# Placing every operand tile and the identity matrix at multiples of 256 bytes in a hybrid encoder kernel

## The chip, the core and the metric

The kernel runs on one core of one Trainium2 chip. The metric is the device time of one launch in microseconds (us), as the median of the runs shown. The engines are called PE (TensorE matmul), PEld (its weight loads), DVE (VectorE), ACT (ScalarE), POOL (GpSimd) and SP (SyncE, which issues the DMAs).

## The reference

One layer of an encoder trunk, run for two batches with the same weights: a prompt of 512 tokens and a sample of 1024 tokens, model width 1024, all in fp32.

```
def _trunk(x, ...):
    h = _rmsnorm(x, norm_attn_g)
    z = h @ w_in                                   # q, k, v, ca, cb
    a_out = _window_attn(q, k, v, bias, band, sink)  # 8 heads of 64, 2 kv heads, |q-k| <= 128
    c = ca * jax.nn.sigmoid(cb)
    c = _dwconv(c, conv_dw_w, conv_dw_b)           # 31 taps, centred, 512 channels
    c = jax.nn.silu(_layernorm(c, conv_ln_g, conv_ln_b))
    x = x + jnp.concatenate([a_out, c], axis=-1) @ w_out
    h = _rmsnorm(x, norm_ffn_g)
    u = _dwconv(h @ w_up, ffn_dw_w, ffn_dw_b)      # 3 taps, 2 * 2816 channels
    x = x + (jax.nn.silu(u[..., :D_FF]) * u[..., D_FF:]) @ w_down
    return _rmsnorm(x, norm_final_g)
```

## The kernel before

**The arithmetic.** Each fp32 operand of a large product is split into a high part in fp32r (the format that PE streams) and a low part, the remainder. A product is then three matmuls into the same PSUM bank: high times high, high times low, low times high. These are the triples of lines L250, L251 and L253 (`proj`, projections by `w_in` and the prompt's up projection), L638 to L640 (`out_half`, output projection), L810 to L812 (down projection of the prompt), L1042 to L1044 (`prod`, up projection of the sample) and L1351 to L1353 (`mm_down`, down projection of the sample). Nearly all have 512 moving columns. The sample's feed-forward part is written as a Strassen-like scheme of seven block products. L501 are the attention scores, with 256 or 384 columns. L175, L184, L209, L354, L543, L602, L614 and L965 are transposes on PE: data as the stationary operand, the identity matrix `ident` as the moving one (L184 transposes the identity itself, to keep PE active at the start).

**The stages.** Up to about 370 us: projections by `w_in` for prompt and sample, with attention and the depthwise convolution beside them. Then, to about 830 us, the prompt's feed-forward part, with the sample's attention and the rest of its convolution beside it. Then the sample's output projection and transposes, from about 910 us its up projection, and from about 1340 us its down projection and the final norm.

**Memory.** SBUF is given out by a class `Slots`: named slots of fixed sizes, each a tile of a pool with the slot's name as its tag, taken by the smallest size that fits and returned when the holder is dropped. Class q has 15 slots of 4096 bytes per partition, h 61 of 2048, c 4 of 4224, d 2 of 2176, s 32 of 64 (statistics and scalars, of which an instruction uses a few columns). A slot gets its address when it is first used, one behind the other; so an s slot taken between two h slots moves all that follow. Ahead of them lie the constants: `ident`, `nhalf`, `warm`, `vecs` (norm weights and biases as columns), `rs2`, `cvw` and `fw` (taps), `sinkb`, `nsink`, `rb`.

```
        fits = [s for s in self.free if s[1] >= need and (among is None or s[0][0] in among)]
        ...
        least = min(s[1] for s in fits)
        slot = next(s for s in fits if s[1] == least)
```

The addresses modulo 256 that come of it in the kernel before (an address is the byte offset within a partition; columns within a tile start at multiples of 512 bytes from it, for all large matmuls):

| tiles | count | address modulo 256, before | after |
|---|---|---|---|
| q (raw weights, split weights, rows of x) | 15 | 160 | 0 |
| h (high and low parts, 512 columns) | 61 | 160 (48), 32 (7), 96 (3), 224 (3) | 0 |
| c (padded rows of the sample, later split weights) | 4 | 32 (3), 160 (1) | 0 |
| d (padded rows of the prompt) | 2 | 160, 224 | 0 |
| ident | 1 | 128 | 0 |
| vecs | 1 | 192 | 0 |
| s | 32 | all multiples of 32 | all multiples of 32 |

Of the 6069 matmuls with 512 columns in fp32r, 4179 have both operands at 160; by stage the share is 77 to 89% up to 800 us and 53 to 61% after it.

**What sets the order.** A scheduler orders the instructions up to the sample's feed-forward part; from there PE's order, and at the end SP's too, is the order of the code. The convolution (L293, `conv_items`) reads its padded input at a shift of one column, 4 bytes, per tap: 24 to 27 taps on DVE, the others as products on ACT and sums on POOL.

Of the kernel before, what the change touches and what calls it, by code (L numbers as in the profile page):

```python
# [9 lines left out]
F32 = mybir.dt.float32  # L10
# [5 lines left out]
P = 128  # L16
# [4 lines left out]
NH = 8  # L21
# [5 lines left out]
PAD = CK // 2  # L27
# [69 lines left out]
def tile_hybrid_encoder(ctx: ExitStack, tc: tile.TileContext, xs, rel_bias, norm_attn_g, w_in,  # L97
                        attn_sink, conv_dw_w, conv_dw_b, conv_ln_g, conv_ln_b, w_out, norm_ffn_g,
                        w_up, ffn_dw_w, ffn_dw_b, w_down, norm_final_g, onehot, outs):
    nc = tc.nc  # L100
    cst = ctx.enter_context(tc.tile_pool(name="cst", bufs=1))
    big = ctx.enter_context(tc.tile_pool(name="big", bufs=1))
    dr = ctx.enter_context(tc.tile_pool(name="dr", bufs=1, space=bass.MemoryType.DRAM))
    ps_guards = [tc.tile_pool(name=f"ps{i}", bufs=1, space=bass.MemoryType.PSUM) for i in range(4)]
    ps = [guard.__enter__() for guard in ps_guards]
    two_of = dict(a0=0, a1=0, a2=1, u0=1, u1=2, b0=2, b1=3, c0=3)

    sb = Slots(big, dict(q=(15, 4096), c=(4, 4224), h=(61, 2048), d=(2, 2176), s=(32, 64)))
    banks = Slots(lambda tag: ps[two_of[tag]], dict(a=(3, 2048), u=(2, 2048), b=(2, 2048), c=(1, 2048)))
    use = dict(step="aub", turn="aub", conv="c", attn="au", norm="b", out="b", up="u", down="b")  # L110

# [3 lines left out]
    def bank(job):  # L115
        return banks.tile([NT], among=use[job])

    GR = [dict(g=0, nN=1, nb=4, x=xs[0], o=outs[0], T=512), dict(g=1, nN=2, nb=8, x=xs[1], o=outs[1], T=1024)]

    ident = cst.tile([P, P], F32, name="ident")  # L120
    nhalf = cst.tile([P, 1], F32, name="nhalf")
    nc.gpsimd.memset(nhalf[:], -0.5)
    warm = cst.tile([P, 1], F32, name="warm")
    nc.scalar.activation(warm[:], nhalf[:], AF.Exp)

    def rstd_of(ss, n, out):
# [41 lines left out]
    def rows_T(parts, out):  # L168
        r = sb.tile([P])
        n = 0  # L170
        for src, k in parts:
            nc.sync.dma_start(r[n:n + k, :], src)
            n += k
        pt = bank("step")
        nc.tensor.transpose(pt[:, :n], r[:n, :], ident[:n, :n])  # L175
        nc.vector.tensor_copy(out, pt[:, :n])

    rw = lambda v: v.rearrange("o (k p) -> (o k) p", p=P)
    vecs = cst.tile([P, 72], F32, name="vecs")
    rows_T([(rw(norm_attn_g), 8)], vecs[:, 0:8])  # L180
    for _ in range(NW // 4):
        pt = bank("step")
# [125 lines left out]
    def evac(kind, c, nt, src):  # L308
        g, n = (0, 0) if nt == 0 else (1, nt - 1)
        T = GR[g]["T"]  # L310
        cols = slice(n * NT, (n + 1) * NT)
        if kind == "cb":
            t = sb.tile([NT])
            nc.scalar.activation(t[:], src, AF.Tanh, scale=0.5)
            tanh_t[nt, c] = t
        elif kind == "ca":
            if n == 0:
                cp = sb.tile([T + 2 * PAD])
                nc.gpsimd.memset(cp[:, 0:PAD], 0.0)
                nc.gpsimd.memset(cp[:, PAD + T:2 * PAD + T], 0.0)  # L320
                cpads[g, c] = cp
            cp = cpads[g, c]
            nc.vector.scalar_tensor_tensor(cp[:, PAD + n * NT:PAD + (n + 1) * NT], tanh_t.pop((nt, c))[:], 1.0, src,  # L323
                                           op0=ALU.add, op1=ALU.mult)
        elif kind == "q":
            hi, lo = sb.tile([NT], F32R), sb.tile([NT], F32R)
            nc.scalar.activation(hi[:], src, AF.Identity, scale=QSCALE)
            nc.vector.scalar_tensor_tensor(lo[:], src, QSCALE, hi[:].bitcast(F32),
                                           op0=ALU.mult, op1=ALU.subtract)
            for e in range(2):  # L330
                for L, s in ((0, hi), (1, lo)):
                    nc.sync.dma_start(
                        qsd[nt][:, L * HD:(L + 1) * HD, 2 * c + e, :].rearrange("b p t -> p b t"),
                        s[e * HD:(e + 1) * HD, :].bitcast(F32).rearrange("p (b t) -> p b t", t=P))
        elif kind == "k":
            hi, lo = sb.tile([NT], F32R), sb.tile([NT], F32R)
            nc.scalar.copy(hi[:], src)
            nc.vector.tensor_tensor(lo[:], src, hi[:].bitcast(F32), op=ALU.subtract)
            for kv in range(NKV):
                if g == 0:  # L340
                    kt[0, kv] = [sb.tile([T], F32R) for _ in range(2)]
                for L, s in ((0, hi), (1, lo)):
                    src_k = s[kv * HD:(kv + 1) * HD, :].bitcast(F32)
                    if g == 0:
                        for half in range(2):
                            nc.sync.dma_start(kt[0, kv][L][half * HD:(half + 1) * HD, :].bitcast(F32), src_k)
                    else:
                        nc.sync.dma_start(ksd[:, kv, L, cols], src_k)
        else:
            vs = sb.tile([NT])  # L350
            nc.scalar.copy(vs[:], src)
            pt = bank("step")
            for i in range(4):
                nc.tensor.transpose(pt[:, i * P:(i + 1) * P], vs[:, i * P:(i + 1) * P], ident[:])  # L354
            src = pt[:].rearrange("p (b c) -> p b c", c=P)
            vs = []
            for kv in range(NKV):
                v = sb.tile([4, P], F32R)
                head = slice(kv * HD, (kv + 1) * HD)
                rest = slice((1 - kv) * HD, (2 - kv) * HD)  # L360
                nc.scalar.copy(v[:, :, head], src[:, :, head])
                nc.vector.tensor_tensor(v[:, :, rest], src[:, :, head], v[:, :, head].bitcast(F32), op=ALU.subtract)
                if g == 1:
                    nc.sync.dma_start(vsd[:, n, kv], v[:].bitcast(F32))
                vs.append(v)
            if g == 0:
                vt[0] = vs
# [16 lines left out]
    def step(i, nt):  # L384
        kind, c, col = order[i]
        pp = bank("step")
        proj(pp[:], ws[i], h1[nt], i < 2 and nt == 0)
        evac(kind, c, nt, pp[:])
        if kind == "ca" and nt != 1:
            g = 0 if nt == 0 else 1  # L390
            (convs, late)[g].append(conv_items(g, c, cpads.pop((g, c))))
        tick()
# [10 lines left out]

    cvw = cst.tile([P, CK * 4], F32, name="cvw")
    fw = cst.tile([P, 132], F32, name="fw")
    sinkb = cst.tile([P, NH], F32, name="sinkb")
    nsink = cst.tile([P, NH], F32, name="nsink")

    def constants():
        rows_T([(rw(norm_ffn_g), 8), (rw(conv_dw_b), 4), (rw(conv_ln_g), 4), (rw(conv_ln_b), 4),  # L410
# [1156 lines left out]
```

## Time and profile before

| | |
|---|---|
| median of 3 runs | 1574.7 us (1574.6 to 1577.9) |
| span of the profiled execution | 1572.4 us (the page gives no other time for it) |
| PE busy | 1526.1 us, 97% |
| PEld busy | 1239.3 us, 79% |
| DVE busy | 1180.7 us, 75% |
| ACT, POOL busy | 801.3 us, 745.2 us |
| mean granted clock of PE | 0.992 |
| DMA | 207.62 MB, 42% of 16 engines |

Busy time of PE is the union of its matmuls. They overlap: the record of one lasts some 393 ns, while the next starts some 230 ns after it. So the pace of matmuls is read from one start to the next, or from the count of weight loads (one for each matmul) in a window in which PE does not idle. In the views, a line of the timeline gives start and duration in us, engine, line, operation, tiles (written <- read, buffer numbers left out: h is any h slot, w, u, a, b are PSUM banks) and shapes. A line of a tile or source view gives the count, then minimum/median/maximum in ns. A line of waits gives who waited for whom, us in total, times, and the longest in us.

### The profile page before, as it was taken

How to read it: one execution, taken by the hardware profiler on the slowest of the kernel's cores; microseconds unless marked ns; L12 is line 12 of the kernel's file. 1: busy time of each engine (PE TensorE's matmuls, PEld its weight loads, DVE VectorE, ACT ScalarE, POOL GpSimd, SP SyncE). 2: the span in 40 equal slices, each digit the busy share in tenths (PEclk: the TensorE clock that was granted, in tenths of full speed). 3: DMA queues.
4: the chain of work that ended last, by engine and by line, in shares of the span. 5: the costliest groups of instructions: out<-in, count | busy, mean ns of one | idle time of the engine just before them, and what ended most of it. 6: DMA issues, size and time to landing. Idle time of an engine off the chain costs nothing. (4 is left out here: it accounts for less than half of the span.)

```text
span 1572.4 us, 20204 instructions
## 1 busy us (share of the span) xinstructions
PE 1526.1 (97%) x6909; PEld 1239.3 (79%) x6909; DVE 1180.7 (75%) x1659; ACT 801.3 (51%) x1402; POOL 745.2 (47%) x655
## 2 busy tenths in 40 slices
PE   8999898998999999999999999999999999999998
PEld 6788777886878877888778887888888878788886
DVE  7999757647869996657575777777787777877794
ACT  4635654335466665655554354454444445554364
POOL 7652334317677777556562333555555454000235
PEclk9999999999999999999999999999999999999999
DMA  7583244427333233323658132333333332594642
GB/s 227 158 207 98 74 121 115 146 78 211 108 103 106 83 118 105 110 88 110 182 156 269 54 94 75 100 100 101 101 100 102 100 114 88 201 367 142 220 142 107
DMA packets 209771, 207.62 MB, mean 132 GB/s; under 512 B 11156, under 2 KB 150748, under 8 KB 209541
## 3 DMA queue, kind: packets, MB, share of 16 engines
q1 hardware_dynamic: 209669, 206.35, 42.0%
q8 instruction: 54, 0.88, 0.2%
q14 instruction: 48, 0.39, 0.1%
HBM read 158.84 MB, written 48.51 MB: 132 GB/s over the span
## 5 line engine op out<-in xcount | busy, mean ns | idle before, releaser
L144 POOL TENSOR_TENSOR q<-q,q 128x1024 fp32r<-128x1024 f32 x72 | 174.7, 2430 | 85.1 <-ACT q L143 51.7
L918 POOL TENSOR_TENSOR q<-q,q 128x512 fp32r<-128x512 f32 x82 | 115.0, 1413 | 155.9 <-ACT q L1028 152.4
L251 PE MATMUL u<-h,q 128*128 128x512 f32 x400 | 159.0, 398 | 0.4 <-DVE h L212 0.4
L250 PE MATMUL u<-h,q 128*128 128x512 f32 x400 | 158.2, 396 | 1.0 <-DVE h L212 0.9
L253 PE MATMUL u<-h,q 128*128 128x512 f32 x384 | 152.2, 397 | 1.1 <-POOL q L144 1.1
L1042 PE MATMUL w<-h,q 128*128 128x512 f32 x372 | 147.4, 396 | 2.5 <-ACT h L1123 1.5
L1044 PE MATMUL w<-h,q 128*128 128x512 f32 x372 | 145.6, 392 | 0.6 <-POOL q L918 0.6
L293 DVE SCALAR_TENSOR_TENSOR c<-c,cvw,c 128x512 f32<-128x512 f32 x184 | 138.0, 750 | 2.7
L1043 PE MATMUL w<-h,q 128*128 128x512 f32 x350 | 137.7, 393 | 0.0
L143 ACT CAST q<-q 128x1024 fp32r<-128x1024 f32 x72 | 75.6, 1050 | 101.3 <-POOL q L144 46.7
L915 POOL TENSOR_TENSOR q<-q,q 128x1024 f32<-128x1024 f32 x8 | 23.9, 2999 | 181.7 <-DVE q L915 170.4
L250 PE MATMUL b<-h,q 128*128 128x512 f32 x256 | 102.8, 402 | 4.4 <-DVE d L323 2.9
L1351 PE MATMUL w<-h,h 128*128 128x512 f32 x264 | 103.7, 393 | 0.0
L1353 PE MATMUL w<-h,h 128*128 128x512 f32 x264 | 103.6, 392 | 0.0
L253 PE MATMUL b<-h,q 128*128 128x512 f32 x256 | 102.0, 399 | 0.9 <-POOL q L144 0.9
L251 PE MATMUL b<-h,q 128*128 128x512 f32 x256 | 102.0, 399 | 0.0
L918 DVE TENSOR_TENSOR h<-h,h 128x512 fp32r<-128x512 f32 (+1 forms) x128 | 92.3, 763 | 11.4 <-ACT h L922 8.7
L918 POOL TENSOR_TENSOR c<-q,c 128x512 fp32r<-128x512 f32 x46 | 71.9, 1576 | 50.9 <-ACT c L1028 50.9
L1352 PE MATMUL w<-h,h 128*128 128x512 f32 x244 | 95.9, 393 | 0.0
L250 PEld LDWEIGHTS u<-h,q 128*128 128x128 f32 x400 | 75.8, 189 | 17.8 <-DVE h L212 1.1
L251 PEld LDWEIGHTS u<-h,q 128*128 128x128 f32 x400 | 75.7, 189 | 17.1 <-DVE h L212 2.2
L922 ACT CAST h<-h 128x512 fp32r<-128x512 f32 x101 | 59.1, 619 | 57.8 <-DVE h L918 23.6
(456 smaller groups left out, 4275.0 us busy)
## 6 DMA issues: line engine op xcount, KB each, us to landing
q<-in_w_up SPq DMA_DIRECT2D x88, 512.0 KB
h<-in_w_down SPq DMA_DIRECT2D x90, 256.0 KB
ga<-q SPq DMA_DIRECT2D x64, 256.0 KB
h<-ga SPq DMA_DIRECT2D x57, 256.0 KB
q<-in_w_in SPq DMA_DIRECT2D x28, 512.0 KB
q<-in_x_sample SPq DMA_DIRECT2D x15, 512.0 KB
h<-qsd SPq DMA_DIRECT2D x24, 256.0 KB
q<-ga SPq DMA_DIRECT2D x20, 256.0 KB
```

The source lines that it names most:

```text
L144: (nc.vector if dve else nc.gpsimd).tensor_tensor(lo[:], raw[:], hi[:].bitcast(F32), op=ALU.subtract)
L250: nc.tensor.matmul(out, whi[:, kc, :], hi[:], start=(kc == 0), stop=False)
L251: nc.tensor.matmul(out, whi[:, kc, :], lo[:], start=False, stop=False)
L253: nc.tensor.matmul(out, wlo[:, kc, :], hi[:], start=False, stop=(kc == KC - 1))
L293: nc.vector.scalar_tensor_tensor(acc[:], src(t), w(t), acc[:], op0=ALU.mult, op1=ALU.add)
L918: (eng or nc.vector).tensor_tensor(out, a, b, op=ALU.subtract)
L1042: nc.tensor.matmul(out, whi[:, s], hi[:], start=(start and c == 0), stop=False, **go)
L1043: nc.tensor.matmul(out, whi[:, s], lo[:], start=False, stop=False, **go)
L1044: nc.tensor.matmul(out, wlo[:, s], hi[:], start=False, stop=(stop and c == 3), **go)
L1351: nc.tensor.matmul(out, sh[:, c], th[:], start=(p == 0), stop=False)
L1352: nc.tensor.matmul(out, sh[:, c], tl[:], start=False, stop=False)
L1353: nc.tensor.matmul(out, sl[:, c], th[:], start=False, stop=(p == NPAIR - 1))
```

## The change

Three things, all in the placing of SBUF tiles:

- The s slots get a pool of their own, `sml`, ahead of the pool of the large slots, so that no small slot lies between large ones.
- The sizes of the c and d slots grow from 4224 to 4352 and from 2176 to 2304 bytes, multiples of 256; the padded rows of the convolution are asked for with 64 columns beyond their tokens instead of 30. `vecs` grows from 72 to 96 columns.
- `nhalf`, `warm`, `sinkb` and `nsink` are declared ahead of `ident`, so that the constants ahead of it fill up to a multiple of 256.

```
+    sml = ctx.enter_context(tc.tile_pool(name="sml", bufs=1))
     big = ctx.enter_context(tc.tile_pool(name="big", bufs=1))
...
-    sb = Slots(big, dict(q=(15, 4096), c=(4, 4224), h=(61, 2048), d=(2, 2176), s=(32, 64)))
+    sb = Slots(lambda tag: sml if tag[0] == "s" else big,
+               dict(q=(15, 4096), c=(4, 4352), h=(61, 2048), d=(2, 2304), s=(32, 64)))
...
+    nhalf = cst.tile([P, 1], F32, name="nhalf")
+    warm = cst.tile([P, 1], F32, name="warm")
+    sinkb = cst.tile([P, NH], F32, name="sinkb")
+    nsink = cst.tile([P, NH], F32, name="nsink")
     ident = cst.tile([P, P], F32, name="ident")
-    nhalf = cst.tile([P, 1], F32, name="nhalf")
...
-    warm = cst.tile([P, 1], F32, name="warm")
...
-    vecs = cst.tile([P, 72], F32, name="vecs")
+    vecs = cst.tile([P, 96], F32, name="vecs")
...
-                cp = sb.tile([T + 2 * PAD])
+                cp = sb.tile([T + 64])
...
-    sinkb = cst.tile([P, NH], F32, name="sinkb")
-    nsink = cst.tile([P, NH], F32, name="nsink")
```

On each of the five engines the program of the change has the same instructions in the same order with the same waits, and each tile sits in the slot of the same name. Only the addresses differ, as the table above gives them.

## The prediction

> **What bounds the kernel now.** I read the page first (busy time, slices, chain), then the windows of 200 us, then the timeline of PE matmul by matmul, then the waits of PE, and last the views of single lines and tiles. The page:
>
> ```profile
> span 1572.4 us, 20204 instructions
> PE 1526.1 (97%) x6909; PEld 1239.3 (79%) x6909; DVE 1180.7 (75%) x1659; ACT 801.3 (51%) x1402; POOL 745.2 (47%) x655
> DVE  7999757647869996657575777777787777877794
> PEclk9999999999999999999999999999999999999999
> PE 34%; DVE 2%; DMA 1%; ACT 1%; issue 0%; POOL 0%; SPq 0%; POOLq 0%; DVEq 0%; ACTq 0%
> q1 hardware_dynamic: 209669, 206.35, 42.0%
> ```
>
> PE is the bound: 1526.1 of 1572.4 us, at the full granted clock, and PE leads the chain. So 46.3 us at most are PE's idle time; the rest is the pace of its matmuls. DVE is nearly full in 7 of the 40 slices (the nines), elsewhere it has room. The profile's page has no time of its own beside the span; the median of the runs, 1574.7, is 2.3 us above the span, and I carry these 2.3 us along. About 0.2% (3 us) is what a measurement here can tell from no change.
>
> An address enters the kernel's time only where an instruction's duration depends on it, since the program of the change has the same instructions, waits and slots in the same order. So the question is which durations depend on addresses. The first is the pace of matmuls with 512 columns, 6069 of the 6909. Three windows (columns: length, then busy us and count of PE, PEld, DVE, ACT, POOL, then clock, DMA share, GB/s):
>
> ```profile
> 94.72:105.61 10.89, 10.89 (x50) 9.01 (x48) 9.72 (x15) 4.12 (x7) 4.95 (x3) 1.00 0.80 184
> 1476.76:1487.87 11.11, 11.11 (x49) 9.02 (x48) 8.40 (x9) 4.99 (x9) 3.36 (x2) 1.00 0.61 196
> 1000.00:1200.00 200.00, 200.00 (x866) 162.00 (x865) 155.23 (x145) 97.32 (x142) 106.45 (x72) 1.00 0.30 99
> ```
>
> PE never idles in any of them, and the weight loads count the matmuls: 10.89/48 = 226.9 ns each in the first, 11.11/48 = 231.5 ns in the second, 200/865 = 231.2 ns in the third. By the slot table, all 48 matmuls of the first have both operands at 160 modulo 256, but only 12 of the 48 in the second. The first has the busier DMA and DVE, so contention is not the reason. Over the whole trace I took the interval from each 512-column matmul's start to the next start, where its neighbours on both sides have 512 columns too and the interval is below 250 ns: 2600 whose own and neighbours' operands all lie at 160 (first and last in the first two rows below) average 228.9 ns, the other 3005 (last two rows) 231.5 ns. All 5847 intervals below 250 ns average 230.4 ns.
>
> ```profile
> 17.81 0.39 PE L251 MATMUL u<-h,q 128*128 128x512 f32 x1
> 1561.31 0.39 PE L1352 MATMUL w<-h,h 128*128 128x512 f32 x1
> 115.58 0.39 PE L253 MATMUL b<-h,q 128*128 128x512 f32 x1
> 1564.33 0.39 PE L1353 MATMUL w<-h,h 128*128 128x512 f32 x1
> ```
>
> **The change part by part.**
>
> *Operand tiles to one residue.* It is the only term of size. The mixture of residues 160, 224, 32 and 96 becomes 0 everywhere. If only equality counts, each matmul moves to the pace of the uniform ones. Lower end: 228.9, the mean with equal direct neighbours, gives (230.4 - 228.9) x 5847 = 8.8 us. Upper end: 226.9, the first window's, gives 3.5 x 5847 = 20.5 us. I take 227.8, midway between the two, since long equal stretches are what the change makes but even these are broken by transposes and waits: 2.6 x 5847 = 15.2 us of PE time.
>
> Not all of it reaches the end. Where DVE is full, PE would only wait more:
>
> ```profile
> 40.00:80.00 40.00, 36.27 (x184) 29.59 (x183) 39.27 (x55) 24.54 (x37) 26.47 (x24) 0.96 0.52 155
> 0.00:200.00 200.00, 184.10 (x879) 149.86 (x880) 173.34 (x283) 101.40 (x187) 99.56 (x114) 0.98 0.52 152
> ```
>
> From 40 to 80 us DVE is busy for 39.27 of 40. The nines are 7 of 40 slices, 17% of the span; but there the share of uniform matmuls is already 77 to 89% (0 to 600 us) against 53 to 61% after 800 us, where PE never idles and DVE has 155 of 200. So less than a fifth of the saving lies in those slices. I let 13 of 15.2 us pass (85%), ends 6.8 (0.77 of 8.8) and 19 (0.93 of 20.5). What is late next there is DVE, with its products for PE.
>
> *Identity matrix, from 128 to 0 modulo 256.* Weight loads of the identity itself and of data tiles at 160, both for transposes:
>
> ```profile
> L184 PEld LDWEIGHTS a<-ident x20: 139/142/230, 1.5 to 9.6; 128*128 128x128 f32 x20
> L209 PEld LDWEIGHTS a<-ident,q x80: 138/141/231, 9.7 to 367.4; 128*128 128x128 f32 x80
> ```
>
> Medians 142 and 141 ns: nothing to gain. On the moving side the identity feeds 640 transposes of 128 columns; at the 2.6 ns above that is 1.7 us, the upper end, and 0 the lower. I take 0, by the rows; the work is on PE, and nothing hides it.
>
> *DVE, ACT and POOL operands.* The depthwise convolution reads its input at every shift of 4 bytes (tap t of L293 starts 4t bytes further), a natural trial of alignment:
>
> ```profile
> L293 DVE SCALAR_TENSOR_TENSOR c<-c,cvw,c x184: 725/750/757, 181.2 to 599.2; 128x512 f32<-128x512 f32 x184
> L293 DVE SCALAR_TENSOR_TENSOR c<-d,cvw,c x78: 735/756/757, 41.4 to 169.9; 128x512 f32<-128x512 f32 x78
> ```
>
> Minimum and maximum are 4% apart over all shifts: no alignment matters to DVE. I take 0 for the three engines, by these rows; the ends are 1% of the time of the slices in which DVE is full, 0.01 x 275 = 3 us either way.
>
> *DMA, small slots, padding, moved declarations.* The same bytes move in the same packets. PE waits on DMA little in all:
>
> ```profile
> PE u L501 <- DMA h<-qsd: 2.8, 2, 2.4
> PE a L501 <- DMA q<-ksd: 2.5, 1, 2.5
> PE a L602 <- DMA h<-cvd: 1.1, 1, 1.1
> ```
>
> That is 6.4 us. Shorter packets could take back a tenth of it, 0.6 us; DMA is at 42%, so PE's own backlog hides the rest. I take 0, ends -1 and +1. The small slots hold scalars and statistics, and keep their width of 64 bytes; the padding and the order of declarations issue nothing.
>
> Sum: 1572.4 - 13 = 1559.4 span, plus 2.3 = 1561.7, so 1562 us.
>
> **The rivals.**
>
> *A larger gain: the whole fixed part of a matmul goes.* In scores with 256 columns four matmuls follow each other at once:
>
> ```profile
> 728.95 0.64 PE L501 MATMUL a<-q,h 128*128 128x256 f32 x4
> 729.43 0.40 PE L250 MATMUL u<-h,q 128*128 128x512 f32 x1
> ```
>
> Start to start it is 0.48 us for 4, 120 ns each. With 226.9 ns for 512 columns that makes 0.4176 ns a column and 13.1 ns that do not scale. Every fp32r operand of the kernel starts 32 bytes off a multiple of 64. If the 13.1 ns is one more read for an operand that begins inside a line, it goes at residue 0: 213.8 ns a matmul, 16.6 x 5847 = 97 us of PE time. PE would then leave DVE behind in more places (DVE 1180.7 of some 1480), so I let 0.7 pass: 68 us, 1507 us; with half of the 13.1 ns gone, some 1530. For it: the fixed part is the same at both lengths. Against: it may belong to the change of weights, and no operand at a multiple of 64 and full rate exists in the trace. The Trainium skill, "TensorE: Matmul & The Clock Gate", section Back-to-back issue gap, gives N / 2.4 + 2.5 ns, 215.8 ns for 512 columns; by that page this rival's pace is the normal one, while no window here is below 226.9 ns.
>
> *No change.* The residue is a mark of the stage and not the cause, or 0 is as mixed as before because a higher part of the address counts. Then 1574.7, between 1572 and 1577. Against: in each of the eight windows of 200 us the uniform ones of the intervals counted above are the faster, by 0.9 to 3.7 ns; for: the 0.9 and 1.1 ns fall between 1000 and 1400 us, where most is to be had, and 296 of the 2600 uniform ones still take 235 to 237 ns. The Trainium skill, "SBUF — State Buffer", section Specifications (TRN2), speaks for this rival: lines are 16 bytes, and every operand before starts at a multiple of 32, so nothing could be gained; the two windows above speak against it.
>
> *Slower: weights and moving operand collide from the first byte.* PE loads the next weights while it streams, and with everything at 0 both reads could begin in the same part of memory. The price is the step seen within uniform matmuls, from 226.9 to 236 ns: (236 - 230.4) x 5847 = 33 us, 1607 us; it decides once more than 4 in 10 matmuls take that step ((230.4 - 226.9)/9.1). Against: with both at 160 they begin equally close today, and that stretch is the fastest.
>
> **How the numbers follow.** Forecast (uniform pace): 0.46, own range 1552 to 1572 (1574.7 less 19 and 6.8 us, with 1 us for DMA and 3 us for DVE). Larger gain: 0.26, 1490 to 1545 around 1507. No change: 0.16. Slower: 0.12. The range 1505 to 1577 leaves out the lower half of the larger gain (0.13) and the slower cases above 1577 (0.07). Faster by over 0.2%: 0.46 + 0.26, 0.72 in all; within 0.2%: 0.15; slower: 0.13.
>
> **What would show it.** In the trace after, the window from 1000 to 1200 us should hold about 878 weight loads (200/0.2278) instead of 865; 930 would mean the larger gain, 865 no change, 850 or less the collision. L293 should keep 750 to 756 ns, L184 and L209 their 141. PE's idle time should grow by 2 us or so, ended by DVE. I am wrong if the pace stays mixed with equal residues, or if the pace improves and the span does not, which would put the bound on DVE over more than its nine slices.

## The result and the profile after

The change makes the kernel faster: 1556.8 us median (1554.4 to 1557.6, 4 runs) against 1576.3 (1574.6 to 1579.4, 4 runs) of the kernel before, a ratio of 0.9878 with a 95% interval of 0.9859 to 0.9898. The forecast was 1562 us, with 1552 to 1572 as the likeliest case's own range. In a later session the same kernel gave 1559.2 us and 0.9901 [0.9884, 0.9917].

The page of the kernel after (lines of the code are 4 further for L1xx to L3xx and 2 further behind them, so L293 is now L297):

```profile
span 1554.2 us, 20204 instructions
PE 1508.0 (97%) x6909; PEld 1236.7 (80%) x6909; DVE 1179.0 (76%) x1659; ACT 799.6 (51%) x1402; POOL 743.5 (48%) x655
DVE  7999857647979996657575767777787877887795
q1 hardware_dynamic: 209669, 206.35, 41.5%
DVE 0%; issue 0%; POOLq 0%; POOL 0%; ACT 0%
```

PE is still the bound. Its busy time fell by 18.1 us (1526.1 to 1508.0) and the span by 18.2 us; what lies between them, PE's idle time, is 46.2 us as before. The chain of waits broke off in the last microseconds and tells nothing here, so the windows have to do. The window from 1000 to 1200 us, and the slice in which DVE was fullest:

```profile
1000.00:1200.00 200.00, 199.80 (x877) 163.90 (x876) 159.61 (x149) 97.87 (x146) 109.99 (x73) 1.00 0.32 105
40.00:80.00 40.00, 34.90 (x184) 28.21 (x183) 39.38 (x56) 24.44 (x37) 26.53 (x24) 1.00 0.50 156
```

876 weight loads stand in the first where 865 stood. In the second nothing is gained: 183 weight loads in both kernels, since DVE is busy for 39.38 of 40 us. From start to start, the 5849 intervals of 512-column matmuls below 250 ns average 227.6 ns (before: 5847 at 230.4), and 4769 of them last 226 or 227 ns (before: 1805). Setting the same interval of both traces side by side, in PE's order, splits the gain: those that changed by less than 25 ns give 16.4 us, those that changed by more 2.6 us. The latter are waits, and matmuls in short stretches in which the granted clock was 0.50 (multiples of some 3.4 us; the window from 40 to 80 us, at 0.96 before and 1.00 after, held one before). PE worked 18.6 us at this half clock before and 11.9 us after, which is an estimated 3 us of its busy time. These stretches differ between executions of one kernel: a second trace of the kernel after has 18.0 us of them, at the same span of 1554.2 us. So the trace puts nearly all of the gain into the pace. The experiments show that this is only half of the story.

The other rows that the prediction went by: DVE's convolution, the transposes' weight loads, and PE's waits on DMA.

```profile
L297 DVE SCALAR_TENSOR_TENSOR c<-c,cvw,c x184: 720/750/757, 180.6 to 593.6; 128x512 f32<-128x512 f32 x184
L188 PEld LDWEIGHTS a<-ident x20: 139/142/231, 1.5 to 9.5; 128*128 128x128 f32 x20
L213 PEld LDWEIGHTS a<-ident,q x80: 138/140/144, 9.6 to 365.9; 128*128 128x128 f32 x80
PE u L503 <- DMA h<-qsd: 2.9, 1, 2.9
PE a L604 <- DMA h<-cvd: 1.5, 1, 1.5
PE a L503 <- DMA q<-ksd: 0.9, 1, 0.9
```

750 ns and 142 and 140 ns are the medians of before within 1 ns; PE's waits on DMA went from 6.4 to 5.3 us.

### The profile page after: what moved, and what is told of

It reads as the page before. It is cut to its first block, busy times and chain, and to the rows that moved or that the text cites. A ratio compares the mean times of both kernels' runs of the same rounds, so it can differ in the third digit from the quotient of the medians.

```text
span 1554.2 us, 20204 instructions
## 1 busy us (share of the span) xinstructions
PE 1508.0 (97%) x6909; PEld 1236.7 (80%) x6909; DVE 1179.0 (76%) x1659; ACT 799.6 (51%) x1402; POOL 743.5 (48%) x655
## 3 DMA queue, kind: packets, MB, share of 16 engines
q1 hardware_dynamic: 209669, 206.35, 41.5%
## 5 line engine op out<-in xcount | busy, mean ns | idle before, releaser
L1044 PE MATMUL w<-h,q 128*128 128x512 f32 x372 | 146.3, 393 | 3.3 <-ACT h L1125 1.9
L297 DVE SCALAR_TENSOR_TENSOR c<-c,cvw,c 128x512 f32<-128x512 f32 x184 | 138.0, 750 | 2.7
```

The costliest lines, as they stand in the source:

```text
L297: nc.vector.scalar_tensor_tensor(acc[:], src(t), w(t), acc[:], op0=ALU.mult, op1=ALU.add)
L1044: nc.tensor.matmul(out, whi[:, s], hi[:], start=(start and c == 0), stop=False, **go)
```

## The experiments

**Theories.** E: what counts is that the operands of successive matmuls share a residue, whichever. Z: residue 0 itself counts. And, once E stood: where the waits come from that a common residue other than 0 brings.

**1. Matmuls by themselves.** A kernel of groups of 96 matmuls back to back, each with its own weights, 24 moving operands and 12 weights in turn, at chosen residues:

```
+    ("m160", 512, mv(160), z),            # name, columns, moving residues, weights' residues (z: all 0)
+    ("m0_64", 512, mv(0, 64), z),
+            nc.tensor.matmul(pt[:, :n], W[:, b:b + P], M[:, a:a + n], start=(k == 0), stop=(k == NMM - 1))
```

> A kernel of its own: 30 groups of 96 back-to-back matmuls, each with its own weight load, their operands' addresses chosen group by group; it computes nothing of the reference's, and its time isn't compared with it, only the interval from one matmul's start to the next, read group by group. Theory E (what counts is that successive moving operands start at the same place within an address period): 226.7 ns for 512 columns in every group in which all moving operands share a residue, whether it is 0, 16 or 160; groups in which they alternate between 0 and 64 mod 256 cost some 10 ns more a matmul (a single operand off by 64 cost about 20 ns in two steps in the trace of before), those between 0 and 128 some 3 ns more (6 ns in two steps). Theory Z (residue 0 itself is what is fast): 226.7 ns at 0 alone and 230 ns or more in the group at 160. Theory S (the weights' addresses count as much as the moving operand's): the groups that alternate the stationary operand between 0 and 64 cost 5 to 10 ns more, too; if not, only the moving side counts. 256 and 384 columns at equal residues: 120.0 and 173.3 ns. If some sequence of residues falls below 226.7 ns, there is a faster layout than the change's.

Windows of 70 matmuls within a group (the first column behind the window is its length, 70 intervals). In this order, with 512 columns: moving 160 and weights 0; moving 0 and weights 160; both 160; moving alternating 0 and 64, weights 0; both 0:

```profile
47.10:63.50 16.40, 16.40 (x71) 13.19 (x70) 0.00 (x0) 0.00 (x0) 0.00 (x0) 1.00 0.00 0
69.57:85.90 16.33, 16.33 (x71) 13.14 (x70) 0.00 (x0) 0.00 (x0) 0.00 (x0) 1.00 0.00 0
91.85:107.72 15.87, 15.87 (x71) 13.14 (x70) 0.00 (x0) 0.00 (x0) 0.00 (x0) 1.00 0.00 1
135.98:152.19 16.21, 16.21 (x71) 13.13 (x70) 0.00 (x0) 0.00 (x0) 0.00 (x0) 1.00 0.00 0
514.11:529.98 15.87, 15.87 (x72) 13.14 (x71) 0.00 (x0) 0.00 (x0) 0.00 (x0) 1.00 0.00 0
```

16.40/70 = 234.3 ns, 233.3, 226.7, 231.6, 226.7. For the pace, Z is refuted: both at 160 is as fast as both at 0. E holds, with a sharper edge than it had: in the first two groups no operand deviates from its predecessor of the same kind, and they are among the slowest. It is the weights and the moving operand that must share the residue, not only moving operands among themselves. By group means, moving operands alternating between 0 and another residue, with weights at 0, cost 5.0 ns a matmul at 32 and 64, 3.3 at 96, 128 and 224, 6.7 at 160 and nothing at 192; weights alternating between 0 and 64 cost 3.4 ns. So equality is not the whole rule: alternating with 192 is unequal in half of the pairs and costs nothing. My 10 ns for a step by 64 was too much, the 3 ns for 128 right. No group of 512 columns falls below 226.7 ns.

**2. All tiles at 160.** The changed kernel with wider `vecs`, which pushes all slots (not `ident`) 160 bytes on:

```
-    vecs = cst.tile([P, 96], F32, name="vecs")
+    vecs = cst.tile([P, 136], F32, name="vecs")
```

> The changed kernel with every operand tile (not the identity) 160 bytes further: all at 160 mod 256. Theory E (equal residues count, whichever): within 0.2% of the changed kernel, 1554 to 1560 us, ratio to before 0.988; the 512-column interval stays at 227.6 ns. Theory Z (residue 0 counts): back to about 1575 us, ratio 1.0, interval 230 ns.

Measured: 1566.6 us, ratio 0.9931 [0.9915, 0.9947], between the two expectations. Its page, and the window from 1000 to 1200 us:

```profile
span 1564.9 us, 20204 instructions
PE 1511.4 (97%) x6909; PEld 1239.0 (79%) x6909; DVE 1178.4 (75%) x1659; ACT 799.1 (51%) x1402; POOL 739.8 (47%) x655
q1 hardware_dynamic: 209669, 206.35, 42.3%
1000.00:1200.00 200.00, 198.29 (x870) 162.62 (x869) 156.88 (x146) 98.15 (x144) 103.34 (x71) 1.00 0.32 102
```

The pace is 227.64 ns, that of the changed kernel, so E is right about the pace inside the kernel, too. But PE idles for 53.5 us instead of 46.2: the time that the pace gives is partly lost in waits. Set beside the changed kernel interval by interval, small differences sum to 0.4 us and large ones to 9.2 us; they are scattered over stage changes and DMA waits, the largest 1.2 us (ahead of L559, at 769 us).

**3 and 4. Half of the tiles 64 or 128 bytes off.** Filler between slots h35 and h36 (64 shown, or 128):

```
         self.free.remove(slot)
+        if slot[0] == "h36" and not self.fill:
+            self.fill = self.pool("h36").tile([P, 64 // 4], F32, tag="fill", name="fill", bufs=1)
```

> The changed kernel with 64 bytes of filler ahead of slot h36, so that h36 to h60 and c lie at 64 mod 256 and all else at 0. Of the 6070 matmuls with 512 columns 1980 (before: 1956, of which 1111 by 64 and 845 by 128) follow one whose moving operand lies at the other residue. Theory E with a dear 64-byte step: 1980 steps at 10 to 13 ns = 20 to 26 us more than the changed kernel, 1576 to 1583 us, so as slow as before or slower, ratio 1.000 to 1.005. If a period of 64 bytes is all that counts: 1557 us, ratio 0.988.

> As the run with half the tiles 64 bytes off, with 128 bytes of filler: the same 1980 steps, now between 0 and 128 mod 256. If 128 bytes is the period that counts: 1557 us, ratio 0.988. If steps by 128 cost the 3 ns that single deviating operands cost in before's trace: 1980 x 3 = 6 us, 1562 us, ratio 0.991. If a step by 128 costs what one by 64 does: 1576 to 1583 us, ratio 1.000 to 1.005.

Measured: 1571.3 us, ratio 0.9973 [0.9957, 0.9988], and 1571.0 us, 0.9968 [0.9953, 0.9982]. The pace is 230.97 and 230.62 ns, 3.4 and 3.0 ns above the changed kernel: spread over the 1980 steps, 10 and 9 ns each. The 10 ns for a step by 64 holds, the 3 ns for one by 128 does not: a step by 128 costs nearly the same, so neither 64 nor 128 bytes is the period. After experiment 1 the count to take is another: by the slots' addresses, weights and moving operand lie at different residues in some 1810 of the 512-column matmuls of the kernel before, 2350 in each of these two, and 1200 in experiment 8. The loss of pace against the changed kernel is 9.0, 8.4, 7.5 and 7.6 ns for each of them. Not only they lose: the prediction's 2600 matmuls with equal operands in themselves and their direct neighbours took 228.9 ns, not 227.6, which suggests that an unequal pair also slows matmuls around it; how far that reaches is not shown. Yet both kernels are faster than the kernel before, whose pace was 230.38. With all q slots still at 0, PE idles less:

```profile
PE 1526.6 (97%) x6909; PEld 1238.0 (79%) x6909; DVE 1182.5 (75%) x1659; ACT 800.5 (51%) x1402; POOL 743.3 (47%) x655
q1 hardware_dynamic: 209669, 206.35, 41.1%
```

(half at 64; its span is 1570.3 us, so 43.7 us of idle against 46.3 before.) In these two runs the DMA engines are less busy than before, in the run with all tiles at 160 as busy as before: 41.1% of 1570.3 us is 645 us, 42.3% of 1564.9 is 662, 42.0% of 1572.4 is 660, and 41.5% of 1554.2, after the change, is 645. The same packets take different times.

**5. Transfers by themselves, and more residues.** The kernel of groups once more; ahead of and beside its first groups run transfers, four at a time, into tiles at chosen residues.

> A kernel of its own again (it computes nothing of the reference's; only intervals and packet times are read). First, transfers alone: 512-byte and 2048-byte rows into tiles, and 2048-byte rows out of them, at 0, 32, 64, 128, 160 and 4 mod 256, four transfers at a time. Theory D (a row that doesn't start at a multiple of 64 bytes costs the DMA engines more): the groups at 32, 160 and 4 have a longer mean packet than those at 0, 64 and 128, by 1 ns or more of the 28.5 ns that a 512-byte packet took in the changed kernel (29.5 in the kernel before and with all at 160). Against it: all groups alike within 0.3 ns. Second, groups of 96 matmuls with all weights at 0 and all moving operands at one other residue, and with both at 16, 32, 64, 128. Theory E2 (what counts is that weights and moving operand share the residue mod 256): both at 16, 32, 64, 128 give 226.7 ns, moving alone at any of 32 to 224 gives 230 to 236. If one offset gives less than 226.7 at 512 columns, or less than 120.0 at 256 and 173.3 at 384, the change's layout isn't the fastest. A cycle of residues as in the kernel before (160, 32, 224, 96; weights at 160): 230 to 233.

Loads in rows of 512 bytes to residues 0, 32, 64 and 128, in this order, and to 0 once more at the end (the last column is GB/s):

```profile
12.60:18.90 6.30, 0.60 (x2) 0.54 (x3) 5.17 (x2) 1.90 (x1) 0.00 (x0) 1.00 1.13 344
18.90:25.80 6.90, 6.90 (x21) 5.49 (x20) 2.26 (x1) 0.00 (x0) 0.00 (x0) 1.00 1.16 302
25.80:33.00 7.20, 7.20 (x34) 5.95 (x32) 0.00 (x0) 0.00 (x0) 0.00 (x0) 1.00 1.17 290
33.10:40.30 7.20, 7.20 (x34) 5.95 (x33) 0.00 (x0) 0.00 (x0) 0.00 (x0) 1.00 1.20 290
83.90:90.20 6.30, 6.30 (x29) 5.10 (x28) 0.69 (x1) 0.00 (x0) 0.00 (x0) 1.00 1.06 311
```

The windows at 0 flatter and understate: the first takes in the end of the load before (333 GB/s by the 512-byte rows alone), the last (311) ends before the group does. The landings are plainer: at 0 the four transfers of 512 KB land 1.53 us apart (343 GB/s) both times, elsewhere 1.70 to 1.83 us apart. The mean packet is 27.0 ns at 0 (27.7 when repeated at the end) and 31.3 to 33.7 at 32, 64, 128, 160 and 4. Theory D as I had put it, that multiples of 64 do, is wrong: 64 and 128 are as slow as 160. Of those tried, only 0 is fast. Rows of 2048 bytes show no such order (88 to 98 ns in, 84 to 89 ns out, the later of two equal groups as far off as different residues).

The matmul groups: both operands at 32, 64 and 128 give 226.7 ns, but both at 16 give 233.3, which I had expected at 226.7; moving operands alone at 32 to 224 give 228.9 to 234.3 ns, the cycle of the kernel before 230.5 (230.4 in the kernel itself). Most of the moving ones ran beside transfers; that did them nothing: 234.3 ns at 160, as without transfers in experiment 1. 512 columns never go below 226.7. Which unequal residues cost how much has no order that these groups show: all moving operands at 192 cost 6.5 ns, where alternating with 0 cost none; all at 64 cost 2.3, where alternating cost 5.0. With 384 columns, moving operands at 32, 64, 160 and 224 cost nothing, and with 256 columns an offset even helps. In the order of the lines: 512 columns, moving at 128 and weights at 0; both at 16; both at 64; then 256 columns, both at 0; moving at 192 and weights at 0:

```profile
115.37:131.70 16.33, 16.33 (x71) 13.14 (x70) 0.00 (x0) 0.00 (x0) 0.00 (x0) 1.00 1.02 363
205.02:221.36 16.34, 16.34 (x72) 13.16 (x71) 0.00 (x0) 0.00 (x0) 0.00 (x0) 1.00 1.04 403
249.09:264.96 15.87, 15.87 (x72) 13.14 (x70) 0.00 (x0) 0.00 (x0) 0.00 (x0) 1.00 0.00 0
334.64:343.04 8.40, 8.40 (x73) 8.40 (x72) 0.00 (x0) 0.00 (x0) 0.00 (x0) 1.00 0.00 0
402.81:410.75 7.94, 7.94 (x73) 7.94 (x71) 0.00 (x0) 0.00 (x0) 0.00 (x0) 1.00 0.01 2
```

For 256 columns that is 120.0 against 113.4 ns. The kernel has 64 such matmuls, 0.4 us in all, so no layout was built on that.

**6 and 7. All tiles at 32, all at 64.** As experiment 2, with `vecs` of 104 and 112 columns.

> The changed kernel with all operand tiles 32 bytes further, at 32 mod 256. The run with all at 160 kept the pace of the changed kernel (227.64 against 227.60 ns) but lost 9 us in waits, while its 512-byte DMA packets went from 28.5 to 29.5 ns. Theory D (those waits come from transfers at odd multiples of 32 bytes): the same again, 1563 to 1569 us, ratio 0.993, packets 29.5 ns. Theory R (residue 160 was slow by itself, or the run's noise): 1554 to 1560 us, ratio 0.988.

> The changed kernel with all operand tiles 64 bytes further, at 64 mod 256. Theory D (64 bytes is what the transfers need, one common residue what the matmuls need): as fast as the changed kernel, 1554 to 1560 us, ratio 0.988, packets 28.5 ns, pace 227.6 ns. If multiples of 256 bytes matter to something else: 1563 to 1569 us, ratio 0.993.

Measured: 1566.2 us, 0.9949 [0.9932, 0.9965], and 1566.0 us, 0.9945 [0.9927, 0.9964], with a pace of 227.56 and 227.58 ns, idle times of 54.1 and 56.2 us and a mean 512-byte packet of 29.2 ns in both. All at 64 was expected as fast as the changed kernel and is not. The three common residues other than 0 agree: the pace comes, and some 7 to 10 us of it are lost in waits. All at 64, to be read like the pages above:

```profile
PE 1510.2 (96%) x6909; PEld 1237.7 (79%) x6909; DVE 1179.7 (75%) x1659; ACT 798.9 (51%) x1402; POOL 739.3 (47%) x655
q1 hardware_dynamic: 209669, 206.35, 42.0%
1000.00:1200.00 200.00, 198.27 (x870) 162.63 (x869) 156.11 (x144) 98.69 (x144) 103.14 (x71) 1.00 0.30 100
PE u L503 <- DMA h<-qsd: 4.7, 2, 3.0
PE w L1044 <- ACT w L1116: 3.0, 4, 1.1
```

PE's waits on `h<-qsd` are 4.7 us instead of 2.9, and a wait on ACT in the sample's up projection (L1044) 3.0 us instead of 0.3. All of PE's waits that a landing ends sum to 7.3, 8.9 and 7.5 us with all at 160, 32 and 64, against 5.3 us in both traces of the changed kernel, so only 2 to 4 us of the lost time are direct waits for a transfer. Slower work of the other engines it is not: DVE is busy for 1178.4 to 1179.7 us in all five traces, ACT for 798.9 to 801.3, and POOL for 739.3 to 745.2 at the three other residues against 743.5 and 748.0 at 0.

**8. The pool alone.** The kernel before, with the small slots in their own pool and no padding:

```
+    sml = ctx.enter_context(tc.tile_pool(name="sml", bufs=1))
-    sb = Slots(big, dict(...))
+    sb = Slots(lambda tag: sml if tag[0] == "s" else big, dict(...))
```

> The kernel before with the small slots in a pool of their own, and none of the padding: 8 of the 61 h slots and half of c lie at 32 mod 256, everything else at 160; 1128 steps by 128 from one moving operand to the next, none by 64. Half the tiles at 128 had 1980 such steps and 230.62 ns, so 227.6 + 3.0 x 1128 / 1980 = 229.3 ns, 10 us more than the changed kernel, and by theory D another 8 us for transfers at 160: about 1574 us, ratio 0.999. Without theory D: 1566 us, 0.994. If the pool of small slots were what counts (small accesses out of the operands' way): 1557 us, 0.988.

Measured: 1571.5 us, 0.9979 [0.9961, 0.9998], pace 229.16 ns (229.3 expected), packet 29.5 ns. The 1.2 ns of pace are 7 us of PE time, and 4 us of them arrive. The pool alone is a small part of the change; the padding is needed.

**9. The changed kernel again,** beside the next three on one chip, since it stood in another session than the layouts at 32, 64 and 160.

> The changed kernel unaltered, on the same chip as the three runs beside it, since the layouts at 160, 32 and 64 (all at the changed kernel's pace of 227.6 ns, all near 1566 us) are to be set against it by less than one per cent: 1554 to 1559 us, ratio 0.986 to 0.990. If it comes out near 1566 us (0.994), the 9 us between it and those three were the chip or the day, and no second effect needs explaining.

Measured: 1559.2 us (1556.0 to 1559.9), 0.9901 [0.9884, 0.9917], pace 227.60 ns, idle 44.6 us. Its interval lies below those of all at 32 and all at 64 and touches that of all at 160 only at its end. So residue 0 is worth some 0.4% beyond the common pace. The comparison goes through the kernel before, run beside each: this chip is another than those of the layouts at 32, 64 and 160.

**10 and 11. Only the rows of 512 bytes moved.** Five q slots become slots of 4352 bytes for the raw blocks of `w_in` and `w_up`; in one kernel the rows land at 0, in the other 64 bytes further:

```
+        o = 16 * new                      # 0 in the first kernel; new: a slot of 4352 bytes was free
+        self.t = self.held.t[:, o:o + KC * P].rearrange("p (k c) -> p k c", c=P)
```

> The changed kernel with five of the q slots as slots of 4352 bytes, which take the raw blocks of w_in and w_up (28 and 82 of their 88 transfers, in rows of 512 bytes); everything still at 0 mod 256, other slots are taken in another order. By itself it tells nothing but what that costs: 1554 to 1575 us. It is the base for the run with the rows at 64.

> As the run with the rows at 0, instruction for instruction, but the 110 transfers' rows land 64 bytes further in their slots, at 64 mod 256 (and ScalarE and GpSimd read them there); every matmul operand stays at 0. Theory D256 (512-byte rows land slower anywhere but at a multiple of 256: 27.0 against 32 to 34 ns alone; and that is what the layouts at 32, 64 and 160 lose): 5 to 10 us more than the run with the rows at 0, mean 512-byte packet 29.2 against 28.5 ns, pace the same. Rival (slower rows are hidden, and the layouts lose elsewhere): within 2 us of it.

Measured: rows at 0, 1562.1 us (1557.6 to 1563.5), 0.9918 [0.9901, 0.9934]; rows at 64, 1564.7 us (1557.5 to 1567.1), 0.9934 [0.9914, 0.9955]. The pace is 227.63 ns in both, the mean packet 28.3 and 28.7 ns, the idle time 49.2 and 50.9 us. The sign is the expected one, but 2.6 us are less than the 5 to 10, and the intervals overlap; in the two traced runs the order is the reverse (spans of 1560.3 and 1558.8 us). That the moved rows cost anything is not shown, and they do not account for the whole 7 to 10 us: their packets lengthened by 0.4 ns only, against 0.7 to 1.1 in the layouts at 32, 64 and 160.

**12. The identity back at 128.** Its declaration ahead of the small constants again, everything else where the change has it:

```
+    ident = cst.tile([P, P], F32, name="ident")
     nhalf = cst.tile([P, 1], F32, name="nhalf")
...
-    ident = cst.tile([P, P], F32, name="ident")
```

> The changed kernel with the identity back at 128 mod 256, all else where it was. 640 transposes read it as one of their operands; if it has to share the other operand's residue as the 512-column matmuls' operands do (3 to 7 ns each), 2 to 4.5 us more than the changed kernel; the prediction's zero: within 1.7 us.

Measured: 1558.9 us, 0.9903 [0.9884, 0.9921], against 1559.2 and 0.9901 beside it. The identity's place is worth nothing that can be measured.

The layouts of the operand tiles in one table. Pace: mean interval of 512-column matmuls below 250 ns. Idle: span less PE busy. Packet: mean of the 137,544 DMA packets of 512 bytes. Small, large: sum of the differences to the changed kernel's trace, interval by interval, of less and of more than 25 ns.

| layout | pace, ns | idle, us | packet, ns | small, us | large, us | time, us |
|---|---|---|---|---|---|---|
| before (160, 32, 224, 96) | 230.38 | 46.3 | 29.5 | 16.4 | 2.6 | 1574 to 1576 |
| pool alone (160, some 32) | 229.16 | 52.9 | 29.5 | 9.2 | 7.3 | 1571.5 |
| half of h at 64, q at 0 | 230.97 | 43.7 | 28.4 | 19.9 | -2.8 | 1571.3 |
| half of h at 128, q at 0 | 230.62 | 42.5 | 28.5 | 17.9 | -4.6 | 1571.0 |
| all at 160 | 227.64 | 53.5 | 29.5 | 0.4 | 9.2 | 1566.6 |
| all at 32 | 227.56 | 54.1 | 29.2 | -0.1 | 11.8 | 1566.2 |
| all at 64 | 227.58 | 56.2 | 29.2 | 0.0 | 11.6 | 1566.0 |
| after: all at 0 | 227.60 | 46.2 | 28.5 | | | 1556.8 |
| after, again | 227.60 | 44.6 | 28.4 | 0.2 | -1.2 | 1559.2 |

Read by columns: the pace depends on one residue being common; the packet is short wherever the q slots, in which most rows of 512 bytes land, are at 0; idle time is least where packets are short and the pace is slow, and most where packets are long and the pace is fast.

The large differences hold more than waits. Stretches at half clock that one of two traces has and the other has not make up 6.2 of the 11.8 us with all at 32, 2.2 of 9.2 at 160 and 1.5 of 11.6 at 64. Over all runs the mean granted clock was 0.994 and 0.993 with everything at 0, and 0.991 to 0.992 with everything at 160, 32 or 64; among 17 runs of the kernel before, 0.001 less clock went with 1.5 us more time. By that estimate 2 to 4 of the 7 to 10 us go with the clock. Whether the longer waits bring the lower clock or chance does, no run shows. A difference remains at equal clock: at 0.993, six runs with all at 32 or 64 took 1564.0 to 1569.4 us, one with all at 160 took 1562.7 us, and two of the changed kernel took 1557.6 and 1559.9 us.

## Why the prediction was right, and where not

**The pace.** Right in mechanism and size. Forecast 227.8 ns, measured 227.60; the term of 15.2 us came out as 2.78 x 5847 = 16.3 us. That 227.8 came so near is in part luck: it was chosen about midway between 228.9 and 226.9 (midway is 227.9), not read off. The reading of the uniform stretches of the old trace as the pace of a uniform layout carried it, though it looked at each matmul and its direct neighbours and could not tell weights from moving operands; the first kernel of groups tells them apart: both must agree, with the exceptions found there.

**How much of it arrives.** Wrong by itself, and hidden by the next point. I let 85% pass. Common residues of 32, 64 and 160 bring the pace alone: 16.0 to 16.5 us of PE time, of which 8.4 to 9.5 us reach the end (1574.9 or 1575.5 less 1566.0 to 1566.6), 52 to 58%. The step that failed is the account of what is late next: I counted the slices in which DVE is full. In fact PE's idle time grows by 7 to 10 us, 1.4 to 2.1 us of it behind the last matmul, the rest in pieces of up to 1.3 us, at stage changes, and behind transfers and evictions, most of them outside the slices in which DVE is full.

**DMA.** Mis-sized. I costed it at 0 with ends of 1 us either way, because the same bytes move in the same packets. They do, but 512-byte rows are faster at residue 0 (27.0 against 31.3 to 33.7 ns by themselves), and the layouts with short packets save 15 to 17 us of each DMA engine's time (660 to 645 us). With the layout at 0 the time is 7 to 10 us less than with the layouts that share another residue, 2 to 4 us of which go with the granted clock. That the shorter packets are the cause fits every layout in the table but is not shown: the one direct trial gave 2.6 us with overlapping intervals. What else residue 0 may quicken stays open; it is no matmul of 512 columns (the small differences are 0 within 0.4 us), not the identity, and not the work of DVE, ACT or POOL (experiments 6 and 7).

**PE's idle time,** forecast to grow by 2 us, ended by DVE: it went from 46.3 to 46.2. By the table that reads as two parts that cancel, the faster pace adding to it and residue 0 taking off.

**The zeros.** Identity: right, by its own run. DVE's convolution: right, 750 ns as before. Small slots and padding as such: nothing is seen of them beyond what they do to the large slots' residues.

**The rivals.** The larger gain (213.8 ns without the fixed part) is refuted: at residue 0 the groups hold 226.7 ns for 512 columns, 173.3 for 384 and 120.0 for 256, so the fixed 13.3 ns stay; an operand beginning inside a line was not their cause. The 215.8 ns of the Trainium skill, "TensorE: Matmul & The Clock Gate", section Back-to-back issue gap, was not met either; that section gives it for a single isolated matmul and not, as the prediction read it, as the normal pace of a stream. No group of fp32r matmuls with 512 columns came below 226.7. No change is refuted. The prediction's argument for it from the 16-byte lines of the Trainium skill, "SBUF — State Buffer", section Specifications (TRN2), that operands at multiples of 32 leave nothing to gain, falls with it: moving operands at 160, 64 or 32 and weights at 0 all lie on multiples of 16, and cost 2 to 8 ns more. The collision is refuted as it was put (everything at 0 is the fastest), but its core has something: weights and moving operand do disturb each other, at unequal residues.

Weighed together, the forecast of 1562 us owes its nearness to two errors of opposite sign, some 4 us too much let through and 7 to 10 us of residue 0 not seen. That they offset each other is luck.

## What to carry to other kernels

Where a kernel is bound by back-to-back matmuls, give the tiles of weights and of moving operands one residue modulo 256, and keep odd-sized small tiles out from between them: here 1% of the kernel for a pool and some padding. Of the four common residues tried, 0 was the fastest, and rows of 512 bytes land faster there; that the one is the cause of the other is not shown. And when an instruction stream gets faster by 1%, do not take the busy engine's share as the share that arrives: only the layouts that changed the pace and left the packets nearly as before showed that little more than half of it did.

## What the runs showed of the hardware that I had not expected

- fp32r matmuls back to back, each with its own weights, 512 columns, all operands at one residue of 0, 32, 64, 128 or 160: 226.7 ns. At residue 0, 256 and 384 columns take 120.0 and 173.3 ns. These three are (columns / 32 + 1) x 13.33 ns, but 480 columns took 216.7 ns, where that gives 213.3. In the kernel after, 912 intervals in a row last 226 or 227 ns (down projection of the sample).
- Both operands at 16 mod 256 give 233.3 ns, moving operands at 4 with weights at 0 236.6: the fast pace held at the multiples of 32 that were tried, and not at 16.
- An unequal residue is no loss at every length: with weights at 0 and the moving operand at 192, 256 columns take 113.4 ns instead of 120.0, but 512 columns 233.2 instead of 226.7.
- Loads in rows of 512 bytes, 512 KB at a time: one lands every 1.53 us (343 GB/s) at residue 0, and every 1.70 to 1.83 us (287 to 308 GB/s) at any other that was tried, 64 and 128 among them.
